# A state space scan that makes the outputs of two chunks in one run

## The chip, the cores and the metric

One NeuronCore of a Trainium2 chip runs the whole program. The metric is the device time of one execution in microseconds (us), given as the median of several runs.

## What is computed

The reference is a trunk of two layers on 2048 tokens of width 1024, in float32. The first is a state space layer (Mamba-2), the second attention over a sliding window. Only the first is touched by the change:

```python
z, xbc, dt = split(h @ w_in)                       # z: gate, xbc: x, B and C
xbc = silu(causal_depthwise_conv(xbc, conv_w, conv_b))   # 4 taps
dt = softplus(dt + dt_bias); A = -exp(a_log)
# ssd_chunked, chunks of 128 tokens, 8 groups of 4 heads of 64 channels, state 128
a_cs = cumsum(dt * A)                              # within a chunk
decay = exp(where(causal, a_cs[l] - a_cs[s], -inf))
y_diag = einsum('gls,grls,sgrp->lgrp', C @ B.T, decay, x * dt)
states = einsum('lgn,grl,lgrp->grpn', B, exp(a_cs[-1] - a_cs), x * dt)
h_in = scan over chunks of  h * exp(a_cs[-1]) + states
y_off = einsum('lgn,grpn,grl->lgrp', C, h_in, exp(a_cs))
y = (y_diag + y_off + d_skip * x) * silu(z)        # skip and gate
out = x + rmsnorm(rmsnorm(y) @ w_out)
```

## The kernel before

Float32 products are made as three products of split operands (`mm3`: high by high, low by high, high by low). The state space layer works on half the tokens at a time (1024, `hf`), and in a half on one group of heads after the other (`g`, eight of them). For each group `ssm_proj` makes twelve product tiles `ps` of 128 channels by 512 tokens: two blocks of tokens each for B, C, x0, x1 and the gates z0, z1. Each takes 24 products of 128x512, accumulated in one of four PSUM buffers (tag `pj`), and the weights of a column tile are loaded by SyncE (`wraw`), rounded by ScalarE (`whi`) and subtracted by GpSimd (`wlo`), with two buffers for each. B, C, x0 and x1 then pass the convolution: ScalarE copies the tile to `raw` and makes the last tap with the bias in `acc`, VectorE adds three taps (L747), ScalarE makes a tanh into `sx` (L750) and VectorE forms silu (L751).

Beside the products of a group runs the scan of the group before it, `ssm_scan`, a generator whose steps `interleave` sets evenly between the products: 17 steps for eight chunks. For a chunk, `stage1` transposes x0, x1 and B on TensorE and multiplies B by C (into `pt`), VectorE and ScalarE make from it `xd`, `xw`, `xh`, `bh`, `bl` and the masked decays `dec`, GpSimd `xl`; ScalarE and GpSimd turn the loaded sums `ab` into the decayed C, in place. `stage2` makes the chunk's state (`sps`, three products of 256 columns; then `hd` on GpSimd and `hn` on VectorE) and directly behind it the outputs: 8 products of 64 output channels each into `yt`, in two halves of the partitions. Each of these stands twice in the trace, as its operands are plain float32. VectorE adds the skip (L841) and GpSimd multiplies by the gate (L843), each twice per chunk on 128 columns; every two chunks the result `ysb` is stored to `yT` in DRAM. `ab` of the chunk after next is loaded behind `stage2`.

At the change of halves the next tokens are normalised and transposed (`prep`) beside the last group; behind the last group the last scan runs beside the first two token tiles of the out-projection (`first`, `head`). The order of instructions on each engine is set when the program is built: a scheduling layer of the language reorders what the code issues within its dependencies, and buffers of a pool (`bufs`) decide what waits for what. SyncE issues all loads and stores shown here, in order.

Of the kernel before, what the change touches and what calls it, by code (L numbers as in the profile page):

```python
# [37 lines left out]
AIN = 2560  # L38

# [20 lines left out]
class Trunk:  # L60
# [7 lines left out]
    def consts(self, pool):  # L68
# [3 lines left out]
        self.identr = pool.tile([P, P], F32R, name="identr")  # L72
        nc.vector.tensor_copy(self.identr, self.ident)
# [22 lines left out]
    def prep(self, src, b, wn, hs, rss=None):  # L96
        """Append (hi, lo) to hs: [k % P, k // P, t] of rmsnorm(src)[t, k] * wn."""
# [46 lines left out]
    def split_w(self, src, cols):  # L144
        """Split weights [K, cols] (k on partitions) into tiles hi, lo [P, K // P, cols]."""
# [10 lines left out]
    def rope_tables(self, wp):  # L156
        """cs2 = [cos, cos] and sn2 = [-sin, sin], [token % P, token // P, 16]."""
# [11 lines left out]
        # r = ang - 2 pi n with n = round(ang / 2 pi) and exact products  # L169
# [57 lines left out]
    def out_piece(self, st, ws, src, i, k0, nk, kt, gated):  # L227
        """k tiles k0 .. k0 + nk of the out-projection of tokens i * P .. (i + 1) * P."""
# [27 lines left out]
    def out_finish(self, st, i, xin, xout, pw, gated, rs=None):  # L256
        """xout = xin + rmsnorm(u) * pw, where u is first scaled to unit mean square of its input if gated;
        rs: [P, 1] for the inverse root mean square of xout."""
# [13 lines left out]
        if gated:  # L272
            # s = r1 * (r1^2 * mean(u^2) + eps)^-0.5 with r1 = (mean(y^2) + eps)^-0.5
# [22 lines left out]
    def att(self, ctx, x1, oT, wn, rs1, hs0, wout, sts):  # L296
# [3 lines left out]
        if True:  # L300
# [7 lines left out]
            # tril[i, j] = 1 where j <= i; mprev[j, i] = 1 where j > i  # L308
# [243 lines left out]
    def ssm_consts(self, pool):  # L552
# [16 lines left out]
        # conv weights and bias and the gate norm, halved, one channel per partition  # L569
# [16 lines left out]
    def dt_proj(self, pool, hs, tabs, atd):  # L586
        """dt, decay tables of the 8 chunks of a half."""
# [23 lines left out]
        # softplus(v) = max(v, 0) + log1p(exp(-|v|)), log1p(u) = 2 atanh(u / (2 + u))  # L611
# [24 lines left out]
        # inclusive sums along the chunk, their total, and the decays  # L636
# [15 lines left out]
        # the sums once more, to DRAM, with (chunk, group) as rows of (r, l)  # L652
# [10 lines left out]
    def ssm_proj(self, ap, hs, hf, g, res, preps, dtg, tail, start):  # L663
        """In-projection, convolution and silu of one group, 1024 tokens.

        preps: generators that make the two blocks of hs, for the first group of a half;
        dtg: what makes the half's time steps, run beside it;
        tail: what to run once the first block is used up, beside the last two column tiles;
        start: called after the first products."""
# [37 lines left out]
            # the second block is made beside the first three, B's weights are split once more  # L707
# [4 lines left out]
        for at, (name, s) in enumerate(order):  # L712
# [30 lines left out]
            acc = ap.tile([P, BLK], F32, tag="cacc", name="acc", bufs=2)  # L743
            nc.scalar.activation(acc, ps, AF.Identity, bias=self.cb[:, ct:ct + 1],  # L744
                                 scale=self.cw[:, 3, ct:ct + 1])
            for j in range(3):
                nc.vector.scalar_tensor_tensor(acc, raw[:, j:j + BLK], self.cw[:, j, ct:ct + 1],  # L747
                                               acc, ALU.mult, ALU.add)
            sx = ap.tile([P, BLK], F32, tag=name, name="sx", bufs=4 if name in ("B", "C") else 3)
            nc.scalar.activation(sx, acc, AF.Tanh)  # L750
            nc.vector.scalar_tensor_tensor(sx, sx, 1.0, acc, ALU.add, ALU.mult)  # L751
            res[name, s] = sx

    def ssm_scan(self, sp, yp, tabs, hf, g, res, yT):
# [3 lines left out]
        hprev = self.hsave[g] if hf else None  # L758
        ysb = None

        abs_ = []

        def load(c):
            ab = sp.tile([P, 4, P], F32, tag="ab", name="ab")
            j = c * 8 + g
            nc.sync.dma_start(ab.rearrange("p r l -> p (r l)"), atd[j].partition_broadcast(P))
            abs_.append(ab)

        def stage1(c):
            ab = abs_[c]  # L770
# [10 lines left out]
            xd = sp.tile([P, 4, 64], F32, tag="xd", name="xd")  # L781
# [14 lines left out]
            cbm = sp.tile([P, P], F32, tag="cbm", name="cbm")  # L796
            nc.vector.tensor_tensor(cbm, pt[:, 3, :], self.triu, ALU.mult)
            dec = sp.tile([P, 4, P], F32, tag="dec", name="dec")
# [10 lines left out]
            return xd, (bh, bl, xh, xl), dec, ce  # L809

        def stage2(c, st, hprev, ysb):
            s, o = divmod(c, 4)
            sl = slice(o * P, (o + 1) * P)
            xd, bx, dec, ce = st
            # next state
            sps = yp.tile([P, 256], F32, tag="st", name="sps")
            self.mm3(sps, *bx, True, True)
            hn = self.hsave[g] if (hf == 0 and c == 7) else sp.tile([P, 256], F32, tag="hst", name="hn")
# [7 lines left out]
            # outputs, two heads stacked on partitions  # L826
            yt = yp.tile([P, 2, P], F32, tag="y", name="yt", bufs=2)
            for pr in range(2):
                for e in range(2):
                    r = 2 * pr + e  # L830
                    nc.tensor.matmul(yt[64 * e:64 * e + 64, pr, :], xd[:, r, :], dec[:, r, :],
                                     start=True, stop=ce is None)
                if ce is not None:
                    for e in range(2):
                        r = 2 * pr + e
                        nc.tensor.matmul(yt[64 * e:64 * e + 64, pr, :], hprev[:, 64 * r:64 * r + 64], ce[:, r, :],
                                         start=False, stop=True)
            for pr in range(2):
                xx = res[f"x{pr}", s]
                yv = ysb[:, pr, (o % 2) * P:(o % 2) * P + P]  # L840
                nc.vector.scalar_tensor_tensor(yv, xx[:, sl], self.dch[:, 2 * g + pr:2 * g + pr + 1],  # L841
                                               yt[:, pr, :], ALU.mult, ALU.add)
                nc.gpsimd.tensor_tensor(yv, yv, res[f"z{pr}", s][:, sl], ALU.mult)  # L843
            return hn

        load(0)
        load(1)
        st = stage1(0)
        yield
        for c in range(8):  # L850
            s, o = divmod(c, 4)
            if o % 2 == 0:
                ysb = sp.tile([P, 2, 2 * P], F32, tag="ysb", name="ysb")
            nxt = stage1(c + 1) if c < 7 else None
            yield
            hprev = stage2(c, st, hprev, ysb)
            if c < 6:
                load(c + 2)
            st = nxt
            if o % 2 == 1:  # L860
                t0 = (8 * hf + c - 1) * P
                nc.sync.dma_start(
                    yT[2 * g * P:(2 * g + 2) * P, t0:t0 + 2 * P].rearrange("(a p) t -> p a t", p=P), ysb)
            yield

# [9 lines left out]
    def run(self, ctx):  # L875
# [9 lines left out]
        self.px = self.pool(ctx, "px", 5)  # L885
# [7 lines left out]
        self.cs2 = cp.tile([P, T // P, 16], F32, name="cs2")  # L893
        self.sn2 = cp.tile([P, T // P, 16], F32, name="sn2")

        # state space layer: y (doubled, before its norm), channel-major, to DRAM
        with ExitStack() as actx:
# [22 lines left out]
            def first(scan):  # L920
                """Beside the last column tiles: the last scan on their finished first block, weights."""
# [8 lines left out]
                for _ in range(3):  # L930
                    next(scan)
                    yield
            for hf in range(2):
                tabs = {}
                hs, hnext = hnext, []
                for g in range(NG):
# [11 lines left out]
                    interleave(self.ssm_proj(ap, hs, hf, g, res, preps, dtg, tail, start), cost, side, 17)  # L948
# [76 lines left out]
```

## Time and profile before

| | |
|---|---|
| median of 3 runs | 2611.55 us (2610.59 to 2617.84) |
| the profiled execution, first to last instruction | 2612.3 us |
| TensorE busy | 2563.8 us, 98% |
| VectorE, ScalarE, GpSimd busy | 1701.4, 1267.6 and 1085.8 us |
| state space layer, up to the end of the last scan | 0 to about 1425 us |
| its out-projection, then the attention layer and its out-projection | to about 1760 us, to 2612 us |

No time of the profiled execution beside its span is given; the span is 0.75 us above the median. A matmul's length in the trace reaches from its issue to its last result, and the next one begins before that, so that the distance from one start to the next tells more than the lengths. PE in the rows is TensorE, PEld its weight loads, DVE is VectorE, ACT ScalarE, POOL GpSimd and SPq SyncE's queue of DMA issues. L831 is line 831 of the kernel.

### The profile page before, as it was taken

The numbers are of one execution on the slowest core, as the hardware profiler recorded it, in microseconds if no ns is written. First come the engines' busy times: TensorE is split into PE (matmuls) and PEld (weight loads), VectorE is DVE, ScalarE is ACT, GpSimd is POOL, SyncE is SP. The second block draws the span as 40 slices with busy tenths as digits, with TensorE's granted clock in tenths as the row PEclk, the third lists the DMA queues.
The fourth block names the chain that finished last, engine by engine and source line by source line (L and its number), as shares of the span: only waits on it lengthen the run. The fifth ranks groups of instructions, "written<-read, shape, count | busy, mean of one in ns | idle before, by whom it ended". The sixth has DMA issues, their size and how long they took to land. (4 is left out here: it accounts for less than half of the span.)

```text
span 2612.3 us, 39548 instructions
## 1 busy us (share of the span) xinstructions
PE 2563.8 (98%) x14307; PEld 2125.4 (81%) x14307; DVE 1701.4 (65%) x3612; ACT 1267.6 (49%) x3015; POOL 1085.8 (42%) x1013
## 2 busy tenths in 40 slices
PE   7999999999999999999998999999999999999998
PEld 6878888888777888888886888888888888888787
DVE  6678666776786667766688544457666767667522
ACT  5455555555645555555556322234545555454321
POOL 2465555555455556555566322223222122221222
PEclk9999999999999999999999999999999999999999
DMA  4322222223323222222225332234112121102343
GB/s 125 106 78 73 78 80 72 88 62 88 88 73 119 71 76 81 69 80 78 80 75 175 108 97 97 97 121 136 53 53 57 58 73 53 53 27 65 105 145 121
DMA packets 266659, 224.50 MB, mean 86 GB/s; under 512 B 31136, under 2 KB 229984, under 8 KB 266464
## 3 DMA queue, kind: packets, MB, share of 16 engines
q1 hardware_dynamic: 266464, 221.98, 27.8%
q8 instruction: 113, 1.85, 0.3%
q14 instruction: 82, 0.67, 0.1%
HBM read 179.72 MB, written 42.21 MB: 85 GB/s over the span
## 5 line engine op out<-in xcount | busy, mean ns | idle before, releaser
L91 PE MATMUL ps<-hi,whi 128*128 128x512 f32 (+1 forms) x1808 | 731.4, 405 | 1.0 <-ACT hi L140 1.0
L93 PE MATMUL ps<-hi,wlo 128*128 128x512 f32 (+1 forms) x1808 | 706.8, 391 | 0.9 <-POOL wlo L153 0.9
L92 PE MATMUL ps<-lo,whi 128*128 128x512 f32 (+1 forms) x1808 | 703.1, 389 | 1.1 <-DVE lo L141 1.1
L91 PEld LDWEIGHTS ps<-hi,whi 128*128 128x128 f32 x1808 | 340.8, 189 | 79.1 <-issue 19.0
L93 PEld LDWEIGHTS ps<-hi,wlo 128*128 128x128 f32 x1808 | 340.4, 188 | 76.9 <-POOL wlo L153 1.7
L92 PEld LDWEIGHTS ps<-lo,whi 128*128 128x128 f32 x1808 | 341.7, 189 | 61.0 <-DVE lo L141 1.8
L747 DVE SCALAR_TENSOR_TENSOR acc<-raw,cw,acc 128x512 f32<-128x512 f32 x384 | 344.5, 897 | 21.8 <-ACT acc L744 17.3
L153 POOL TENSOR_TENSOR wlo<-wraw,whi 128x1024 fp32r<-128x1024 f32 x114 | 282.5, 2478 | 133.7 <-ACT whi L151 121.8
L800 ACT ACTIVATE dec<-ab,acs 128x128 f32<-128x128 f32 x512 | 167.3, 392 | 172.1 <-DMA ab<-atd 165.5
L806 POOL TENSOR_TENSOR ab<-ab,sx 128x512 f32<-128x512 f32 x120 | 162.9, 1358 | 195.3 <-ACT ab L805 189.4
L252 PE MATMUL u<-oh,yh 128*128 128x512 f32 x768 | 241.6, 394 | 0.0
L252 PE MATMUL u<-ol,yh 128*128 128x512 f32 x768 | 239.3, 392 | 0.0
L252 PE MATMUL u<-oh,yl 128*128 128x512 f32 x768 | 238.2, 390 | 0.0
L377 POOL TENSOR_TENSOR qs<-qf,qs 128x256 fp32r<-128x256 f32 x64 | 49.3, 770 | 419.2 <-ACT qs L376 387.9
L750 ACT ACTIVATE sx<-acc 128x512 f32<-128x512 f32 x128 | 81.0, 633 | 268.1 <-DVE acc L747 267.9
L236 POOL TENSOR_TENSOR yl<-yr,yh 128x1024 fp32r<-128x1024 f32 (+1 forms) x64 | 118.9, 1858 | 164.9 <-ACT yh L234 164.9
L843 POOL TENSOR_TENSOR ysb<-ysb,zz 128x128 f32<-128x128 f32 x256 | 162.6, 648 | 48.9 <-DVE ysb L841 48.1
L91 PE MATMUL ps<-qh,hi 128*128 128x384 f32 x512 | 177.7, 348 | 0.0
L92 PE MATMUL ps<-ql,hi 128*128 128x384 f32 x512 | 172.9, 338 | 0.9 <-POOL ql L333 0.9
L93 PE MATMUL ps<-qh,lo 128*128 128x384 f32 x512 | 172.3, 337 | 0.0
L252 PEld LDWEIGHTS u<-oh,yl 128*128 128x128 f32 x768 | 144.2, 188 | 32.1 <-issue 0.9
L234 ACT ACTIVATE yh<-yr 128x1024 fp32r<-128x1024 f32 (+1 forms) x64 | 54.1, 846 | 238.7 <-PE u L252 176.4
(217 smaller groups left out, 4827.9 us busy)
## 6 DMA issues: line engine op xcount, KB each, us to landing
wraw<-in_ssm_w_in SPq DMA_DIRECT2D x98, 512.0 KB, 4.0
ab<-atd SPq DMA_DIRECT2D x128, 256.0 KB, 3.2
xt<-in_x SPq DMA_DIRECT2D x32, 512.0 KB, 5.0
yT<-ysb SPq DMA_DIRECT2D x64, 256.0 KB, 2.2
yr<-yT SPq DMA_DIRECT2D x32, 512.0 KB, 4.0
xt<-x SPq DMA_DIRECT2D x32, 512.0 KB, 4.0
oraw<-in_ssm_w_out SPq DMA_DIRECT2D x16, 512.0 KB, 5.9
x<-xt SPq DMA_DIRECT2D x32, 256.0 KB, 2.1
```

What stands on the lines that cost most here:

```text
L91: nc.tensor.matmul(ps, sh, mh, start=first, stop=False)
L92: nc.tensor.matmul(ps, sh, ml, start=False, stop=False)
L93: nc.tensor.matmul(ps, sl, mh, start=False, stop=last)
L153: nc.gpsimd.tensor_tensor(lo, raw, hi.bitcast(F32), ALU.subtract)
L234: nc.scalar.activation(yh, yr, AF.Copy)
L236: nc.gpsimd.tensor_tensor(yl, yr, yh.bitcast(F32), ALU.subtract)
L252: nc.tensor.matmul(st["u"][h], y[:, k, :], w[:, j, 512 * h:512 * h + 512], start=k0 + k == 0 and m == 0, stop=k0 + k == kt - 1 and m == 2)
L747: nc.vector.scalar_tensor_tensor(acc, raw[:, j:j + BLK], self.cw[:, j, ct:ct + 1], acc, ALU.mult, ALU.add)
L750: nc.scalar.activation(sx, acc, AF.Tanh)
L800: nc.scalar.activation(dec[:, r, :], ab[:, r, :], AF.Relu, scale=-1.0, bias=acs[:, c, 4 * g + r:4 * g + r + 1])
L806: nc.gpsimd.tensor_tensor(ce, ce, Ct[:, sl].unsqueeze(1).to_broadcast([P, 4, P]), ALU.mult)
L843: nc.gpsimd.tensor_tensor(yv, yv, res[f"z{pr}", s][:, sl], ALU.mult)
```

## The change

The scan goes by pairs of chunks. `stage2` is divided into `state`, for one chunk, and `outputs`, for two. A pair's steps are: the state of the first chunk with `stage1` two chunks ahead; the same for the second; then the outputs of both into one `yt` of 256 columns, with one skip and one gate for each half of the heads, the store, and the loads of two `ab`. That makes 14 steps. `ab`, `xd` and `dec` get four buffers instead of two, `hn` three, `cbm` one. The convolution accumulates in `sx` itself and puts the tanh into `raw`, so that `acc` is gone. The pool `px` has four buffers instead of five, and the rope tables and `identr` are made in a pool of their own behind the state space layer.

```diff
+SCAN = 14
-            acc = ap.tile([P, BLK], F32, tag="cacc", name="acc", bufs=2)
-            nc.scalar.activation(acc, ps, AF.Identity, bias=self.cb[:, ct:ct + 1],
+            sx = ap.tile([P, BLK], F32, tag=name, name="sx", bufs=4 if name in ("B", "C") else 3)
+            nc.scalar.activation(sx, ps, AF.Identity, bias=self.cb[:, ct:ct + 1],
                                  scale=self.cw[:, 3, ct:ct + 1])
             for j in range(3):
-                nc.vector.scalar_tensor_tensor(acc, raw[:, j:j + BLK], self.cw[:, j, ct:ct + 1],
-                                               acc, ALU.mult, ALU.add)
-            sx = ap.tile([P, BLK], F32, tag=name, name="sx", bufs=4 if name in ("B", "C") else 3)
-            nc.scalar.activation(sx, acc, AF.Tanh)
-            nc.vector.scalar_tensor_tensor(sx, sx, 1.0, acc, ALU.add, ALU.mult)
+                nc.vector.scalar_tensor_tensor(sx, raw[:, j:j + BLK], self.cw[:, j, ct:ct + 1],
+                                               sx, ALU.mult, ALU.add)
+            th = raw[:, 0:BLK]
+            nc.scalar.activation(th, sx, AF.Tanh)
+            nc.vector.scalar_tensor_tensor(sx, th, 1.0, sx, ALU.add, ALU.mult)
             res[name, s] = sx
...
-            xd = sp.tile([P, 4, 64], F32, tag="xd", name="xd")
+            xd = sp.tile([P, 4, 64], F32, tag="xd", name="xd", bufs=4)
...
-            dec = sp.tile([P, 4, P], F32, tag="dec", name="dec")
+            dec = sp.tile([P, 4, P], F32, tag="dec", name="dec", bufs=4)
...
+        def outputs(c0, hps):
+            yt = yp.tile([P, 2, 2 * P], F32, tag="y", name="yt", bufs=2)
+            for u in range(2):
+                xd, _, dec, ce = sts[c0 + u]
+                for pr in range(2):
+                    yo = yt[:, pr, u * P:(u + 1) * P]
                     for e in range(2):
                         r = 2 * pr + e
+                        nc.tensor.matmul(yo[64 * e:64 * e + 64], xd[:, r, :], dec[:, r, :],
+                                         start=True, stop=ce is None)
+                    if ce is not None:
+                        for e in range(2):
+                            r = 2 * pr + e
+                            nc.tensor.matmul(yo[64 * e:64 * e + 64], hps[u][:, 64 * r:64 * r + 64], ce[:, r, :],
+                                             start=False, stop=True)
+            s, o = divmod(c0, 4)
+            sl = slice(o * P, (o + 2) * P)
+            ysb = sp.tile([P, 2, 2 * P], F32, tag="ysb", name="ysb")
             for pr in range(2):
+                yv = ysb[:, pr, :]
+                nc.vector.scalar_tensor_tensor(yv, res[f"x{pr}", s][:, sl], self.dch[:, 2 * g + pr:2 * g + pr + 1],
                                                yt[:, pr, :], ALU.mult, ALU.add)
                 nc.gpsimd.tensor_tensor(yv, yv, res[f"z{pr}", s][:, sl], ALU.mult)
...
+        for c in range(0, 8, 2):
+            h0 = hprev
+            h1 = state(c, h0)
+            stage1(c + 2)
             yield
+            hprev = state(c + 1, h1)
+            stage1(c + 3)
             yield
+            outputs(c, (h0, h1))
+            load(c + 4)
+            load(c + 5)
+            yield
...
-        self.px = self.pool(ctx, "px", 5)
+        self.px = self.pool(ctx, "px", 4)
```

What this moves is read from the written order of both programs. On TensorE, in the middle of a group, the order before has the state of a chunk (`sps`) and its outputs (`yt`) between the products `ps` of the next group:

```order
L93 MATMUL ps<-hi,wlo 128x512
L91 MATMUL sps<-xh,bh 128x256
L92 MATMUL sps<-xl,bh 128x256
L93 MATMUL sps<-xh,bl 128x256
L831 MATMUL yt<-dec,xd 64x128 x2
L836 MATMUL yt<-ab,hn 64x128 x2
L831 MATMUL yt<-dec,xd 64x128 x2
L836 MATMUL yt<-ab,hn 64x128 x2
L91 MATMUL ps<-hi,whi 128x512
```

After the change, at the same place of a group, the outputs of two chunks stand between products `ps`:

```order
L92 MATMUL ps<-hi,wlo 128x512
L833 MATMUL yt<-dec,xd 64x128 x2
L838 MATMUL yt<-ab,hn 64x128 x2
L833 MATMUL yt<-dec,xd 64x128 x2
L838 MATMUL yt<-ab,hn 64x128 x2
L833 MATMUL yt<-dec,xd 64x128 x2
L838 MATMUL yt<-ab,hn 64x128 x2
L833 MATMUL yt<-dec,xd 64x128 x2
L838 MATMUL yt<-ab,hn 64x128 x2
L90 MATMUL ps<-hi,whi 128x512
```

And 18 to 24 products away from them stands the state of one chunk, followed by the transposes of the chunk two further:

```order
L91 MATMUL sps<-xl,bh 128x256
L92 MATMUL sps<-xh,bl 128x256
L776 MATMUL pt<-ident,sx 128x128
L777 MATMUL pt<-ident,sx 128x128
L778 MATMUL pt<-ident,sx 128x128
L779 MATMUL pt<-sx 128x128
L90 MATMUL ps<-hi,whi 128x512
```

Over the whole program the `yt` products stand in 129 runs before and in 66 after (64 pairs, one of them cut into three at the change of halves); `sps` is followed directly by a product of another tile, `ps` or `u`, 8 times before and 31 times after. The number of products is the same. On SyncE's queue, in the steady part of the second half, the order before is (`ab`: decay sums, `wraw`: weights, `yT`: the stored outputs)

```order
L766 DMA ab<-atd_60 128x512
L862 DMA yT<-ysb 128x2x256
L766 DMA ab<-atd_60 128x512
L149 DMA wraw<-in_ssm_w_in 128x8x128
L766 DMA ab<-atd_60 128x512
L862 DMA yT<-ysb 128x2x256
L149 DMA wraw<-in_ssm_w_in 128x8x128
```

and after the change

```order
L148 DMA wraw<-in_ssm_w_in 128x8x128
L764 DMA ab<-atd_60 128x512 x2
L849 DMA yT<-ysb 128x2x256
L148 DMA wraw<-in_ssm_w_in 128x8x128 x2
L764 DMA ab<-atd_60 128x512
```

so that a weight load stands behind two loads of `ab` and a store instead of one or two of these. The ScalarE row of the convolution that writes `sx` for the second block of `x0` (L743 after the change) waits there for VectorE, and the decays of the next two chunks stand behind it.

## Rows read from the trace of the kernel before

**Rows 1.** The page: the span, and section 1, busy time of each engine
```profile
span 2612.3 us, 39548 instructions
...
PE 2563.8 (98%) x14307; PEld 2125.4 (81%) x14307; DVE 1701.4 (65%) x3612; ACT 1267.6 (49%) x3015; POOL 1085.8 (42%) x1013
```

**Rows 2.** Busy time by stage; columns: stretch, length, busy of each engine (instructions)
```profile
200.00:1360.00 1160.00, 1152.27 (x6626) 943.36 (x6626) 826.51 (x1606) 633.57 (x1363) 651.12 (x615) 1.00 0.27 79
...
1425.00:1760.00 335.00, 335.00 (x1494) 275.51 (x1491) 158.59 (x252) 109.80 (x164) 99.24 (x77) 1.00 0.34 109
```

**Rows 3.** TensorE's timeline around one chunk's outputs; columns: start, length, what
```profile
505.89 0.40 PE L93 MATMUL ps<-hi,wlo 128*128 128x512 f32 x1
...
507.94 0.39 PE L93 MATMUL ps<-hi,wlo 128*128 128x512 f32 x1
...
508.28 0.28 PE L92 MATMUL sps<-xl,bh 128*128 128x256 f32 x1
508.40 0.28 PE L93 MATMUL sps<-xh,bl 128*128 128x256 f32 x1
508.61 0.44 PE L831 MATMUL yt<-dec,xd 128*64 128x128 f32 x4
508.88 0.39 PE L836 MATMUL yt<-ab,hn 128*64 128x128 f32 x4
509.10 0.39 PE L831 MATMUL yt<-dec,xd 128*64 128x128 f32 x4
509.31 0.39 PE L836 MATMUL yt<-ab,hn 128*64 128x128 f32 x4
509.63 0.50 PE L91 MATMUL ps<-hi,whi 128*128 128x512 f32 x1
509.97 0.40 PE L92 MATMUL ps<-lo,whi 128*128 128x512 f32 x1
...
511.82 0.39 PE L91 MATMUL ps<-hi,whi 128*128 128x512 f32 x1
```

**Rows 4.** Groups of instructions by shape; columns: count | busy us, mean ns | idle before, releasers
```profile
L843 POOL TENSOR_TENSOR ysb<-ysb,zz 128x128 f32<-128x128 f32 x256 | 162.6, 648 | 48.9 <-DVE ysb L841 48.1
...
L831 PE MATMUL yt<-dec,xd 128*64 128x128 f32 x1024 | 105.6, 286 | 11.8 <-DVE dec L808 8.7 <-DVE ysb L841 3.0
...
L836 PE MATMUL yt<-ab,hn 128*64 128x128 f32 x896 | 87.9, 273 | 0.0
L824 POOL TENSOR_TENSOR hd<-hn,cd 128x256 f32<-128x256 f32 x104 | 87.2, 839 | 120.3 <-DVE hn L825 76.8 <-DVE raw L739 21.2 <-DVE raw L737 19.6
...
L841 DVE SCALAR_TENSOR_TENSOR ysb<-sx,dch,yt 128x128 f32<-128x128 f32 x256 | 80.1, 339 | 19.7 <-PE yt L836 18.6 <-PE yt L831 1.0
...
L287 DVE SCALAR_TENSOR_TENSOR v<-u,s,bc 128x512 f32<-128x512 f32 x64 | 45.1, 747 | 11.2 <-POOL s L87 10.7
...
L836 PE MATMUL yt<-ab,hsave 128*64 128x128 f32 x64 | 6.8, 291 | 0.0
```

**Rows 5.** Timelines of SyncE's queue and of ScalarE: a weight load and its conversion
```profile
502.69 0.37 SPq L149 DMA_DIRECT2D wraw<-in_ssm_w_in  x1
...
522.31 1.06 ACT L151 ACTIVATE whi<-wraw 128x1024 fp32r<-128x1024 f32 x1 [0.36 <-issue]
```

**Rows 6.** TensorE's waits from 0 to 1370 us; columns: total, times, longest
```profile
PE yt L831 <- DVE dec L808: 4.9, 2, 3.4
PE yt L831 <- DVE ysb L841: 3.0, 2, 1.8
...
PE sps L91 <- DVE hn L825: 1.2, 2, 0.6
```

**Rows 7.** TensorE's waits from 1370 to 1426 us, the last scan
```profile
PE yt L831 <- DVE dec L808: 3.8, 3, 2.4
PE sps L91 <- ACT bh L793: 2.2, 2, 2.0
PE sps L92 <- POOL xl L791: 2.0, 3, 1.5
```

More of the change, by code (lines that the diff above doesn't have):

```diff
@@ L757, in ssm_scan @@
         dt, acs, cd, w2, atd = (tabs[k] for k in ("dt", "acs", "cd", "w2", "atd"))
-        hprev = self.hsave[g] if hf else None
-        ysb = None
-        abs_ = []
+        abs_, sts = [], []
         def load(c):
[L764 to L767, printed above, removed]
+            if c < 8:
+                ab = sp.tile([P, 4, P], F32, tag="ab", name="ab", bufs=4)
+                j = c * 8 + g
+                nc.sync.dma_start(ab.rearrange("p r l -> p (r l)"), atd[j].partition_broadcast(P))
+                abs_.append(ab)
         def stage1(c):
+            if c > 7:
+                return
             ab = abs_[c]
@@ L808, in stage1, with state @@
             nc.vector.tensor_tensor(dec, dec, cbm.unsqueeze(1).to_broadcast([P, 4, P]), ALU.mult)
[L809 to L814, printed above, removed]
+            sts.append((xd, (bh, bl, xh, xl), dec, ce))
+        def state(c, hprev):
             sps = yp.tile([P, 256], F32, tag="st", name="sps")
-            self.mm3(sps, *bx, True, True)
-            hn = self.hsave[g] if (hf == 0 and c == 7) else sp.tile([P, 256], F32, tag="hst", name="hn")
+            self.mm3(sps, *sts[c][1], True, True)
+            hn = self.hsave[g] if (hf == 0 and c == 7) else sp.tile([P, 256], F32, tag="hst", name="hn", bufs=3)
             if hprev is None:
@@ L825, in stage2 @@
                 nc.vector.tensor_tensor(hn, hd.rearrange("p h d -> p (h d)"), sps, ALU.add)
[L827 to L833, printed above, removed]
+            return hn
+        def outputs(c0, hps):
[4 more added lines that the diff above has]
+                    yo = yt[:, pr, u * P:(u + 1) * P]
@@ L842, in stage2 @@
                                                yt[:, pr, :], ALU.mult, ALU.add)
                 nc.gpsimd.tensor_tensor(yv, yv, res[f"z{pr}", s][:, sl], ALU.mult)
[L844 to L848, printed above, removed]
-        yield
[L850 to L854, printed above, removed]
-            yield
[L856 to L863, printed above, removed]
+            t0 = (8 * hf + c0) * P
@@ new lines, in outputs @@
+            nc.sync.dma_start(
+                yT[2 * g * P:(2 * g + 2) * P, t0:t0 + 2 * P].rearrange("(a p) t -> p a t", p=P), ysb)
+        for c in range(4):
+            load(c)
+        stage1(0)
+        yield
+        stage1(1)
+        yield
+        hprev = self.hsave[g] if hf else None
+        for c in range(0, 8, 2):
+            h0 = hprev
+            h1 = state(c, h0)
+            stage1(c + 2)
+            yield
+            hprev = state(c + 1, h1)
+            stage1(c + 3)
+            yield
+            outputs(c, (h0, h1))
+            load(c + 4)
+            load(c + 5)
@@ L892, in run @@
         self.gn = cp.tile([P, 16], F32, name="gn")
-        self.cs2 = cp.tile([P, T // P, 16], F32, name="cs2")
-        self.sn2 = cp.tile([P, T // P, 16], F32, name="sn2")
         with ExitStack() as actx:
@@ L929, in first @@
                     yield
-                for _ in range(3):
-                    next(scan)
-                    yield
+                next(scan)
+                yield
             for hf in range(2):
@@ L947, in run @@
                     cost = 56 if g == 0 else 52 if hf and g == NG - 1 else 58
-                    interleave(self.ssm_proj(ap, hs, hf, g, res, preps, dtg, tail, start), cost, side, 17)
+                    interleave(self.ssm_proj(ap, hs, hf, g, res, preps, dtg, tail, start), cost, side, SCAN)
                     if dtg:
@@ L963, in head @@
                 yield from pieces[1]
-            interleave(head(), 15, side, 10)
+            interleave(head(), 15, side, SCAN - 5)
         wn = self.bcast(cp, io["pre_norm"][1], tag="wn")
         rs1 = cp.tile([P, T // P], F32, name="rs1")
+        rope = self.pool(ctx, "rope")
+        self.cs2 = rope.tile([P, T // P, 16], F32, name="cs2")
+        self.sn2 = rope.tile([P, T // P, 16], F32, name="sn2")
+        self.identr = rope.tile([P, P], F32R, name="identr")
+        nc.vector.tensor_copy(self.identr, self.ident)
         hs = []
```

9 lines of the change are left out of this document (1 added, 8 removed).

## The prediction

> **What bounds the kernel now.** I read the page first, then the busy times by stage, then TensorE's timeline inside one stage, then its waits. The page gives a span of 2612.3 us with TensorE busy 98% of it [rows 1]. By stages the change touches only the state space layer, up to about 1425 us; there TensorE is busy 1152.27 of 1160 us in the long middle, while VectorE has 827, ScalarE 634 and GpSimd 651 us [rows 2]. TensorE's stream sets the time, and of the others only what it waits for counts. That stream is not simply full, though. In the timeline [rows 3] one should look at starts, not durations: a 128x512 product lasts 0.39 to 0.40 us, but the next one starts 0.228 us later (507.94 less 505.89, over nine products). Up to 0.16 us can therefore be lost between two products without any idle time being shown. That is what the rows from 508.28 to 509.97 show, when the scan's small products cut into the stream.
>
> **The price of one run of outputs.** A run means the 64-column products into `yt` that follow each other with nothing else between them. Its price is read from [rows 3] in five places. (1) Entry: `sps` products start 0.12 apart, the first `yt` starts 0.21 after the last `sps`: 0.09 lost. (2) The rows with x4 are a quarter of the run each; the second and third take 0.22 and 0.21, the first 0.27 (508.61 to 508.88): 0.05 lost. (3) Exit: the last quarter takes 0.32 until the next `ps` starts (509.31 to 509.63): 0.105 lost. (4) That `ps` is followed 0.34 later instead of 0.228: 0.11 lost. (5) The eight after it take 1.85 us (509.97 to 511.82) instead of 1.82: 0.03. Together 0.385 us, paid per run however long it is, since the quarters in between go at an even pace.
>
> **The change part by part.**
>
> *Outputs of two chunks together.* In the written order 129 runs become 66; the shapes and the number of the products stay ([rows 4]: 1024 records of L831, 896 of L836 and 64 more on the saved state). 63 runs fewer, at 0.385: 24.3 us gained. One piece of this has no row: the entry will mostly come from a 128x512 product, not from `sps`. I take the same 0.09. The bounds are nothing lost there, and a wait for the whole 0.39 us that such a product lasts, thus 0.39 - 0.228 = 0.16. The 129 old runs cost 49.7 us; 66 new ones cost 66 x 0.295 = 19.5 or 66 x 0.455 = 30.0, so the gain is 30.2 at best and 19.7 at worst. The Trainium skill, "TensorEngine Tiling (Array Packing)", section "Tiling Modes", says that changing the tiling mode, and not just the tile, drains the engine. Taken strictly, the entry would wait for the product before it to be finished, the gain would be 4.6 us smaller and the time 2590 instead of 2585. The trace does not bear out the strict reading: `yt` enters 0.21 us after an `sps` that lasts 0.28.
>
> *The state product now stands with the next chunk's transposes, or alone.* `sps` followed by transposes pays nothing new: the transposes' own exit is there before and after. At the end of a scan there is no chunk left to transpose, and `sps` then returns to `ps` by itself: by the order 23 more such returns. The trace has hardly any of them; the nearest rows are items 4 and 5 above, 0.14 us, so 3.3 us lost, bounds 0 and 23 x 0.25 = 5.8 (with an exit like item 3).
>
> *Skip and gate on 256 columns.* VectorE's skip took 339 ns for 128 columns, and the like operation on 512 columns, also from PSUM, 747 [rows 4]; by a straight line between them 475 for 256. 256 x 0.339 becomes 128 x 0.475: 26 us less on VectorE. GpSimd's gate, 256 x 0.648, becomes 128 at some 0.84 (the row of `hd`, 256 columns): 58 us less. Neither engine is full [rows 2], so I put nothing down for it; their earlier ends show in the waits below. If VectorE were the limit the gain would be up to 26 us.
>
> *Convolution in place.* The same number of instructions on the same shapes; what moves is which buffer waits. `raw` is held to the last step (the old `acc` was, with two buffers as well), and `sx` is taken when the first step is written, some 4 us sooner. That makes one new wait: ScalarE's L743 for the second block of `x0` writes where the scan still reads chunks 2 and 3, whose skip comes by the order 12 products (2.7 us) and a run (some 1.9 us) later, plus two skips of 0.475. So ScalarE stands some 6 us once per group. Behind it are the decays of the next chunks and the next evacuation, which TensorE wants three product tiles later: 3 x 24 x 0.228 = 16 us. The wait is hidden with 10 us to spare, so 0.
>
> *Loads.* `ab` is fetched in pairs, and each weight load on SyncE's queue stands behind a pair and a store of `yT`. Weights have room: the load issued at 502.69 us is first read by ScalarE at 522.31 [rows 5], 20 us later. A group's 288 products take 66 us, so with the scan's own a chunk is some 9 to 10 us, and a delay by one chunk stays covered: 0. One `px` buffer fewer and the rope tables moved out of the way touch the out-projections, where TensorE shows 335.00 of 335.00 us busy [rows 2]; a token tile's input would have to come 22 us (96 x 0.228) late before that cover is gone: 0.
>
> *Waits.* TensorE's waits in the scan sum to 9.1 us before 1370 us [rows 6] and 8.0 us in the last scan [rows 7]. The 4.9 us on `dec` are the first outputs of a half, which now come some 54 products after the transposes instead of 15: gone. Of the 4.2 us on the freed `yt` and on `hn` I take back a quarter, as both buffers stay as few. The last scan keeps its 8.0: nine steps stand between fewer products of the out-projection, with fewer runs. 6 us gained; bounds 17.1 gained and 10 lost.
>
> *Sum*, against the profiled execution's 2612.3 us: less 24.3, plus 3.3, less 6.0 gives 2585.3. The median of the runs is 0.75 us lower, so 2585 us, 1.0% less.
>
> **The rivals.** *TensorE is full: only waits can be won.* For it speaks the busy time of 99% in the middle stage [rows 2]; then the lost time at a run's ends would be the small products' own and be paid at other ends, and the time is 2612.3 + 3.3 - 6 or so, 2600 to 2612. Against it are the equal quarters inside the run [rows 3]. The Trainium skill, "Perfetto Trace Analysis", section "Identifying the Most-Contended Engine", calls TensorE's busy share a poor measure of headroom since matmuls are pipelined, and points to the share of weight loads. Here that is 943 of 1160 us [rows 2], which by it leaves room, and the trace agrees.
>
> *The last scan stalls more.* Its two states and the pair's outputs stand six products apart (1.4 us), and the chain from transposes through VectorE, ScalarE and GpSimd to `xl` already ends late there [rows 7]. If each of the three pairs left there waits 4 us more, 12 us go back: 2597.
>
> *Slower: ScalarE's new wait uncovers PSUM.* The four product buffers give 16 us. If the wait on chunks 2 and 3 lasted 20 us instead of 6, each of 15 groups would lose about 4 us, 60 in all, less the 27: 2645. It decides from 16 + 27/15 = 18 us on. Nothing in the waits of before [rows 6] comes near it.
>
> *More than forecast:* all 17.1 us of waits gone and free entries: 2612 - 30 - 17 + 3 = 2568.
>
> That the order does not do what is written is excluded by the order itself, but for one place at the change of halves where a run is cut into three (counted above).
>
> **How the numbers follow.** Forecast (2572 to 2599) 0.66; full TensorE 0.16; last scan 0.08; slower 0.05; more 0.05. A measurement tells about 0.3%, 8 us, from no change, so faster means below 2603.7: 0.66 + 0.07 + 0.05 and a quarter of the full-TensorE case, 0.82. Within: 0.13. Slower: 0.05. The range 2570 to 2605 leaves out most of the full-TensorE case, the slower one and a little below.
>
> **What would show it.** In the profile after: the same counts of `yt` records, in 66 runs, with edges of 0.09, 0.05, 0.105, 0.11 and 0.03 us as before; the stage from 200 to 1360 us shorter by some 20 us at the same work; no waits on `dec` in the first scan of a half; the attention layer unchanged. I am wrong if runs of 32 cost twice the edges of runs of 16, if the entry from `ps` costs 0.16 us more, or if TensorE waits for `ps` buffers or weights in every group.

## The result, and the profile after

The changed kernel takes 2684.5 us (2682.9 to 2687.0, four runs) against 2611.1 us in the runs beside it: 1.0273 times the time, interval 1.026 to 1.0286. Forecast were 2585 us and faster; it is slower by 2.7%. One of the ten runs of e8 below took 9350.7 us at a granted clock of 0.50; the ratios leave it out. The page of the changed kernel, span and section 1:

```profile
span 2681.2 us, 39280 instructions
...
PE 2570.6 (96%) x14307; PEld 2142.0 (80%) x14307; DVE 1707.9 (64%) x3484; ACT 1266.6 (47%) x3015; POOL 1051.0 (39%) x885
```

Against [rows 1] TensorE runs the same 14307 instructions, but it is idle for 2681.2 - 2570.6 = 110.6 us instead of 48.5, and busy for 6.8 us more, where 21 less were expected. Both need a cause. First the edges of a run of outputs, in TensorE's timeline (start, length, what), to be held against [rows 3]:

```profile
499.47 0.39 PE L92 MATMUL ps<-hi,wlo 128*128 128x512 f32 x1
499.79 0.44 PE L833 MATMUL yt<-dec,xd 128*64 128x128 f32 x4
500.06 0.39 PE L838 MATMUL yt<-ab,hn 128*64 128x128 f32 x4
...
501.37 0.39 PE L838 MATMUL yt<-ab,hn 128*64 128x128 f32 x4
501.68 0.50 PE L90 MATMUL ps<-hi,whi 128*128 128x512 f32 x1
502.02 0.40 PE L91 MATMUL ps<-lo,whi 128*128 128x512 f32 x1
```

The entry from a 128x512 product takes 0.32 us from start to start (0.228 + 0.09), the first quarter 0.27, the exit 0.31, the product behind it 0.34, and the quarters between go at an even pace. These are the prices of the prediction, now paid once for two chunks. So the gain is there, and something else took more. TensorE's waits from 0 to 1500 us (total, times, longest):

```profile
PE sps L90 <- DVE hn L821: 74.1, 19, 7.2
```

In [rows 6] this wait had 1.2 us, twice; the waits of `yt` on `dec` and on `ysb` of [rows 6] are gone. One group of the first half shows what it is. Timelines (start, length, engine, what, and the idle time before with its releaser), TensorE first, then SyncE's queue, ScalarE, VectorE and GpSimd:

```profile
505.89 0.28 PE L90 MATMUL sps<-xh,bh 128*128 128x256 f32 x1
...
510.69 0.39 PE L92 MATMUL ps<-hi,wlo 128*128 128x512 f32 x1
515.00 0.55 PE L90 MATMUL sps<-xh,bh 128*128 128x256 f32 x1 [3.92 <-DVE hn L821]
...
503.67 0.37 SPq L148 DMA_DIRECT2D wraw<-in_ssm_w_in  x1
504.13 1.00 SPq L764 DMA_DIRECT2D ab<-atd  x2
...
504.69 0.78 ACT L743 ACTIVATE sx<-ps,cb,cw 128x512 f32<-128x512 f32 x1 [1.84 <-DVE ysb L845]
508.74 1.57 ACT L800 ACTIVATE dec<-ab,acs 128x128 f32<-128x128 f32 x5 [3.28 <-DMA ab<-atd]
510.23 0.57 ACT L739 ACTIVATE raw<-ps 128x512 f32<-128x512 f32 x1
510.70 0.76 ACT L743 ACTIVATE sx<-ps,cb,cw 128x512 f32<-128x512 f32 x1
...
505.50 2.88 DVE L746 SCALAR_TENSOR_TENSOR sx<-raw,cw,sx 128x512 f32<-128x512 f32 x3 [0.46 <-ACT sx L743]
511.50 0.75 DVE L746 SCALAR_TENSOR_TENSOR sx<-raw,cw,sx 128x512 f32<-128x512 f32 x1 [0.50 <-ACT sx L743]
512.77 1.76 DVE L746 SCALAR_TENSOR_TENSOR sx<-raw,cw,sx 128x512 f32<-128x512 f32 x1
514.45 0.41 DVE L821 TENSOR_TENSOR hn<-hd,sps 128x256 f32<-128x256 f32 x1
...
512.58 1.40 POOL L806 TENSOR_TENSOR ab<-ab,sx 128x512 f32<-128x512 f32 x1 [6.32 <-ACT ab L805]
```

Read it backwards. The second state of the pair starts at 515.00, when `hn` of the first, which reads the only `sps` buffer, has run (514.45). `hn` stands on VectorE behind two taps of a convolution tile (511.50 and 512.77, the second 1.76 us long, beside GpSimd's decayed C, L806, late with the same pair of `ab`). Their `raw` and `sx` come from ScalarE at 510.23 and 510.70, behind `dec` of a later chunk, and that waited for `ab` until 508.74. `ab` was issued at 504.13, behind a weight load that had itself waited; and ScalarE had stood 1.84 us for the second block of `x0` before. The first state ran at 505.89, so `hn` came 9.0 us behind its state, while the next state is wanted after 18 products `ps`, 5.2 us (515.00 - 3.92 - 505.89). In the steady groups this happens once per group, at the third pair: some 4 us in the first half, 5 to 7 in the second.

The wait costs more than itself. Busy times by stretch of the same place; the third column from the right is the granted clock:

```profile
505.00:511.00 6.00, 6.00 (x31) 4.84 (x29) 3.02 (x5) 2.72 (x8) 1.26 (x2) 1.00 0.76 216
511.00:514.95 3.95, 0.08 (x1) 0.00 (x0) 3.45 (x5) 3.92 (x9) 1.42 (x2) 0.92 0.00 0
514.95:521.00 6.05, 6.00 (x18) 5.16 (x19) 6.05 (x9) 3.45 (x7) 6.05 (x5) 0.50 0.00 0
521.00:525.00 4.00, 4.00 (x25) 3.05 (x26) 4.00 (x10) 0.58 (x2) 1.53 (x2) 0.98 0.46 131
```

TensorE is called busy from 514.95 to 521, but at 0.50, its lower level of 1.2 GHz: 18 instructions in 6.05 us, against 31 in 6.00 before the wait. From the first product of `sps` to the twelfth `ps` behind it the stalled place takes 6.4 us (515.00 to 521.38), the first state of the same pair 3.4 (505.89 to 509.33): about 2.9 us more per such wait, hidden in the busy time.

### The profile page after: what moved, and what is told of

Same layout as the page of the kernel before. It is cut to its first block, busy times and chain, and to the rows that moved or that the text cites. A ratio compares the mean times of both kernels' runs of the same rounds, so it can differ in the third digit from the quotient of the medians.

```text
span 2681.2 us, 39280 instructions
## 1 busy us (share of the span) xinstructions
PE 2570.6 (96%) x14307; PEld 2142.0 (80%) x14307; DVE 1707.9 (64%) x3484; ACT 1266.6 (47%) x3015; POOL 1051.0 (39%) x885
## 4 chain that ended last, share of the span: by engine, by line
PE 71%; DVE 10%; DMA 5%; ACT 5%; issue 4%; POOL 4%; SPq 0%; ACTq 0%; POOLq 0%; DVEq 0%
PE u L251 18%; PE ps L90 13%; PE ps L91 13%; PE ps L92 13%; DMA ab<-atd 4%; DVE sx L746 4%; PE sc L421 2%; POOL wlo L152 2%; PE yt L833 2%; PE yt L838 1%; PE ot L467 1%; ACT dec L800 1%; PE tt L449 1%; PE tq L388 1%; PE ot L471 1%
## 5 line engine op out<-in xcount | busy, mean ns | idle before, releaser
L746 DVE SCALAR_TENSOR_TENSOR sx<-raw,cw,sx 128x512 f32<-128x512 f32 x384 | 378.0, 985 | 20.2 <-ACT sx L743 17.5
L800 ACT ACTIVATE dec<-ab,acs 128x128 f32<-128x128 f32 x512 | 168.1, 392 | 170.8 <-DMA ab<-atd 160.5
L806 POOL TENSOR_TENSOR ab<-ab,sx 128x512 f32<-128x512 f32 x120 | 166.8, 1390 | 184.5 <-ACT ab L805 181.2
L749 ACT ACTIVATE raw<-sx 128x512 f32<-128x512 f32 x128 | 80.6, 630 | 294.3 <-DVE sx L746 275.6
L847 POOL TENSOR_TENSOR ysb<-ysb,zz 128x256 f32<-128x256 f32 x128 | 111.2, 886 | 153.8 <-DVE ysb L845 153.8
L251 PEld LDWEIGHTS u<-ol,yh 128*128 128x128 f32 x768 | 144.1, 188 | 31.4 <-DVE ol L223 0.7
```

Source lines behind the costliest of these rows:

```text
L251: nc.tensor.matmul(st["u"][h], y[:, k, :], w[:, j, 512 * h:512 * h + 512], start=k0 + k == 0 and m == 0, stop=k0 + k == kt - 1 and m == 2)
L746: nc.vector.scalar_tensor_tensor(sx, raw[:, j:j + BLK], self.cw[:, j, ct:ct + 1], sx, ALU.mult, ALU.add)
L749: nc.scalar.activation(th, sx, AF.Tanh)
L800: nc.scalar.activation(dec[:, r, :], ab[:, r, :], AF.Relu, scale=-1.0, bias=acs[:, c, 4 * g + r:4 * g + r + 1])
L806: nc.gpsimd.tensor_tensor(ce, ce, Ct[:, sl].unsqueeze(1).to_broadcast([P, 4, P]), ALU.mult)
```

## The experiments

Theory A: the second state of a pair has come to stand one step behind the first and waits for its `hn`, which goes behind a convolution tile on VectorE; what makes that tile late (the load of `ab`, its place behind a weight load, the wait for `x0`) adds up. The rivals are that one of these is the cause by itself. All ratios are against the kernel before on the same chip (median 2611.1 us beside the changed kernel, 2614.8 beside the first four runs, 2614.4 beside the next four, 2615.3 beside the last three). TensorE's times and the waits are of one profiled run each.

| run | us | ratio and interval | TensorE busy, idle, us | waits of `sps` on `hn`, us |
|---|---|---|---|---|
| before | 2611.1 | | 2563.8, 48.5 | 1.2 |
| changed | 2684.5 | 1.0273 (1.026 to 1.0286) | 2570.6, 110.6 | 74.1 |
| e1_state_pair | 2685.3 | 1.0263 (1.0244 to 1.0281) | 2572.6, 110.6 | 73.8 |
| e2_ab_five | 2641.0 | 1.0095 (1.0076 to 1.0113) | 2562.0, 79.0 | 45.3 |
| e3_x0_four | 2649.2 | 1.0132 (1.0109 to 1.0154) | 2561.6, 92.7 | 26.3, and 29.8 put down to `dec` |
| e4_weights_other_queue | 2633.0 | 1.0067 (1.0046 to 1.0087) | 2551.2, 79.3 | 36.6 |
| e5_queue_and_ab_five | 2638.3 | 1.0091 (1.0076 to 1.0106) | 2557.1, 81.9 | 41.6 |
| e6_pause_between_states | 2596.1 | 0.9933 (0.9918 to 0.9948) | 2543.1, 48.7 | 10.7 |
| e7_second_state_other_bank | 2628.0 | 1.0054 (1.0038 to 1.0071) | 2552.4, 72.9 | 16.7 |
| e8_in_place_alone | 2618.1 | 1.0012 (1.0003 to 1.0022) | 2565.2, 47.8 | 0.6 |
| e9_pause_behind_outputs | 2678.8 | 1.0255 (1.0238 to 1.0272) | 2562.9, 111.0 | 70.8 |
| e10_queue_ab_x0 | 2607.1 | 0.9976 (0.9967 to 0.9985) | 2544.9, 62.8 | 23.3 |
| e11_pause_and_room | 2592.2 | 0.9921 (0.9904 to 0.9938) | 2539.1, 48.2 | 10.3 |

**Two halves of one tile for a pair's states.**

```diff
-            sps = yp.tile([P, 256], F32, tag="st", name="sps")
+            if c % 2 == 0:
+                stp.append(yp.tile([P, 2, 256], F32, tag="st", name="sps"))
+            sps = stp[-1][:, c % 2, :]
```

> The changed kernel, but the two states of a pair have the two halves of one PSUM tile, so that the second state needn't wait until VectorE has read the first. Theory A (the stall of each group is the second state waiting for the one PSUM buffer of `sps`, which VectorE reads late): the waits of `sps` on `hn`, 74.1 us in the changed kernel, fall below 15 us, TensorE's clock stays up, and the time is 2585 to 2600 us, as the gain at the edges of the runs is then bare. Rival B (the scan as a whole is late, since its inputs are): the stall moves on to the next products of the scan, `yt` or the next pair's `sps`, and the time stays above 2650 us.

Nothing moved, and the trace names the same releaser:

```profile
PE sps L90 <- DVE hn L823: 73.8, 19, 6.3
```

In this kernel's written order too the second state's first product waits for a VectorE instruction. So the edit didn't part the two states, and the run tells nothing of what a buffer of its own would bring; e7 asks that again.

**One contributor at a time.** A fifth buffer for `ab` (room from `ysb`):

```diff
-                ab = sp.tile([P, 4, P], F32, tag="ab", name="ab", bufs=4)
+                ab = sp.tile([P, 4, P], F32, tag="ab", name="ab", bufs=5)
-            ysb = sp.tile([P, 2, 2 * P], F32, tag="ysb", name="ysb")
+            ysb = sp.tile([P, 2, 2 * P], F32, tag="ysb", name="ysb", bufs=1)
```

> The changed kernel with five buffers of `ab` instead of four (and one `ysb` instead of two, to make room). The load of a pair's first chunk no longer waits for the outputs of the pair before. Theory A, with the late `ab` as what starts the chain (ScalarE waits for it, VectorE's taps wait for ScalarE, `hn` stands behind the taps, the second state waits for `hn`): at least half of the 74.1 us of waits of `sps` goes and with it half of the slow clock, so 2610 to 2645 us. Rival C (what starts it is ScalarE's wait for the buffer of the second block of x0): nothing changes, 2680 to 2690 us.

A fourth buffer for `x0`, with the same room:

```diff
-            sx = ap.tile([P, BLK], F32, tag=name, name="sx", bufs=4 if name in ("B", "C") else 3)
+            sx = ap.tile([P, BLK], F32, tag=name, name="sx", bufs=4 if name in ("B", "C", "x0") else 3)
```

> The changed kernel with four buffers for x0 instead of three (and one `ysb` instead of two, to make room). The convolution of the second block of x0 no longer waits for the skip of chunks 2 and 3. Rival C: the stall in each group goes, 2590 to 2620 us. Theory A with the late `ab` at its start: ScalarE only waits for `ab` instead, and the time stays at 2675 to 2690 us.

The weights issued by GpSimd instead of SyncE:

```diff
-        nc.sync.dma_start(raw, src.rearrange("(k p) c -> p k c", p=P))
+        nc.gpsimd.dma_start(raw, src.rearrange("(k p) c -> p k c", p=P))
```

> The changed kernel with the weight loads of a column tile issued by GpSimd instead of SyncE. A pair of `ab` then no longer stands behind a weight load that waits for its buffer; in the trace of the changed kernel that was 2.4 us in the group looked at (501.7 to 504.13 us). Theory A with SyncE's order as the reason why `ab` is late: the stalls become 2 us shorter each, 2630 to 2660 us, if the issue itself costs GpSimd little. If `ab` is late because of its buffers and its own 4 us to land, the time moves by less than 10 us, 2675 to 2690 us.

Each took back a part, 44, 35 and 52 us of 73, and in different places. With five `ab` the second half's waits fell to about 1 us a group and the first half's only to 3.4; with four `x0` the first half's fell to about 2 and the second half's stayed near 5. The profile puts six of the second half's down to `dec`, but there too `hn` ends 0.15 us before the state starts, as in the others, so they count as waits for `hn`. The times with five `ab` and with the other queue lie in theory A's ranges, though five `ab` took only 28.8 us of the waits, less than the half expected; 2649 with four `x0` lies between the two ranges given, so neither the late `ab` nor the wait for `x0` is the cause by itself. That 44, 35 and 52 sum to more than the 73 fits links of one chain better than separate costs. None alone brings the kernel to the time before.

**Queue and `ab` together.**

> Weights fetched by GpSimd's queue and a fifth buffer for ab (one for ysb), both together. Alone they gave 2633 and 2641 us against 2685 of the changed kernel. Theory A (all of it is one chain: late ab, ScalarE, the taps on VectorE, hn, the second state; each piece shortens it): together they take the chain below the 5 us that a step leaves, the second state waits under 10 us in all, granted clock back to 0.995, time 2590 to 2610. Rival (both take away the same microseconds of the load): no more than the better one alone, 2625 to 2640.

The rival's number came: 2638, no better than the queue alone. ScalarE's waits for `ab` had fallen from 160.5 us to 14.1, and still the first half waited 3.0 us a group. What stands there on VectorE and GpSimd:

```profile
504.65 4.29 DVE L746 SCALAR_TENSOR_TENSOR sx<-raw,cw,sx 128x512 f32<-128x512 f32 x3 [0.46 <-ACT sx L743]
...
504.91 1.09 POOL L847 TENSOR_TENSOR ysb<-ysb,zz 128x256 f32<-128x256 f32 x1
505.97 1.27 POOL L806 TENSOR_TENSOR ab<-ab,sx 128x512 f32<-128x512 f32 x1
507.21 1.18 POOL L847 TENSOR_TENSOR ysb<-ysb,zz 128x256 f32<-128x256 f32 x1
```

Three taps take 4.3 us beside three GpSimd instructions in a row, where a tap mostly takes 0.74. The pair's outputs bring two gates of 256 columns at once, and they fall on the taps that stand before `hn`: a fourth contributor. In the changed kernel the same three taps took 2.88 us (505.50), since GpSimd's decayed C (L806), held up by the late `ab`, ran only at 512.58. An earlier `ab` puts it between the gates and onto these taps, so part of what the load gives is taken back.

**An empty step between the states.**

```diff
-SCAN = 14
+SCAN = 18
             h1 = state(c, h0)
             stage1(c + 2)
             yield
+            yield
             hprev = state(c + 1, h1)
```

> One empty step between the two states of a pair, 18 steps a group instead of 14, all else as in the changed kernel: the states of a pair stand two steps (some 9 us) apart instead of one (some 6 us). Theory A (the second state waits for the hn of the first, which is late behind the convolution; the lateness itself, some 10 us from state to hn, was there before as well): the wait is covered up to 9 us, 3 to 4 us of each stall go in the first half and 4 of 6 in the second; 2590 to 2615. Rival (the loads stall the engines and TensorE pays wherever it stands): the stalls move but stay, 2650 to 2685.

2596 us, 0.7% faster than before. The same place of a group, TensorE and VectorE:

```profile
489.36 0.28 PE L90 MATMUL sps<-xh,bh 128*128 128x256 f32 x1
499.22 0.28 PE L90 MATMUL sps<-xh,bh 128*128 128x256 f32 x1
...
497.94 0.41 DVE L821 TENSOR_TENSOR hn<-hd,sps 128x256 f32<-128x256 f32 x1
```

`hn` is as late as in the changed kernel, 9.0 us from the state's start to its own end. But the next state now stands 9.9 us away, and TensorE doesn't wait. (In the second half `hn` also came earlier, at most 7 us behind its state in the steady groups instead of 10 to 12, so that there it isn't the distance alone.) One part of the expectation was wrong: that this lateness had been there before the change. Before, at the latest `hn` of a steady group:

```profile
499.15 0.28 PE L91 MATMUL sps<-xh,bh 128*128 128x256 f32 x1
508.17 0.28 PE L91 MATMUL sps<-xh,bh 128*128 128x256 f32 x1
...
503.80 0.41 DVE L825 TENSOR_TENSOR hn<-hd,sps 128x256 f32<-128x256 f32 x1
```

That is 5.1 us of lateness against 9.0 of distance. The change did both: it made `hn` later and brought the next state nearer.

**The second state in another bank.** In six of eight groups it takes one of the four product buffers:

```diff
-            sps = yp.tile([P, 256], F32, tag="st", name="sps")
+            sps = (self.pp.tile([P, 256], F32, tag="pj", name="sps") if c % 2 and g < 6
+                   else yp.tile([P, 256], F32, tag="st", name="sps"))
```

> In six of eight groups the second state of a pair goes to one of the four product buffers instead of the one buffer of the states, so that it needn't wait until VectorE has read the first. Theory A (the one buffer of sps is what TensorE stops at): 12 of 16 stalls go, what waits next is the outputs a step later, for hn; 2600 to 2630. Rival (ScalarE and VectorE are late for all that TensorE wants, so that the next product buffer isn't free either): the wait comes back within 3 us at ps or at sps itself, with three buffers left for the products; 2665 to 2700.

In a middle group of the first half, TensorE and VectorE:

```profile
479.43 0.28 PE L90 MATMUL sps<-xh,bh 128*128 128x256 f32 x1
484.45 0.28 PE L90 MATMUL sps<-xh,bh 128*128 128x256 f32 x1
...
489.68 0.40 DVE L822 TENSOR_TENSOR hn<-hd,sps 128x256 f32<-128x256 f32 x1
```

The second state starts 5.0 us behind the first, before `hn` has run, and nothing waits. From 200 to 600 us the list of TensorE's waits is empty. That shows that the one buffer of `sps` is what TensorE stopped at. In the second half other waits come in its place (0 to 1500 us):

```profile
PE sps L91 <- POOL xl L791: 10.7, 6, 2.1
...
PE yt L839 <- DVE hn L822: 6.0, 4, 2.0
PE ps L92 <- POOL wlo L152: 5.4, 7, 1.8
```

GpSimd and `hn` are now what comes next; the 16.7 us on `hn` in the table lie in the groups that keep the one buffer and in the last scan. So the time, 2628, is in the range of theory A, at its upper end.

**The convolution in place, alone,** in the kernel before (the diff is the convolution's part of the change).

> The kernel before with nothing but the convolution in place. By the prediction's step the new wait of ScalarE for the second block of x0 is covered: 2611 to 2618, no stall of TensorE over 1 us that was not there. Rival (the wait itself costs, as the 35 us that a fourth buffer for x0 gave back in the changed kernel could mean): 2640 or more. Theory A says that it costs only together with the two states one step apart, so it sides with the first.

2618 us, 1.0012 times before: nothing to speak of. With the states 8 to 10 us apart the new wait is covered.

**The control: the empty step behind the outputs.**

```diff
             load(c + 4)
             load(c + 5)
             yield
+            yield
```

> The control to the pause between the states: the same 18 steps a group, but the empty step stands behind the outputs and loads of a pair, so that the two states stand one step of 4.8 us apart instead of 6.2, and the loads of ab come a step ahead of their use. Theory A (what counts is the distance from a state to the next against the 9 to 10 us that hn takes): the load's share of the lateness goes, as with five buffers for ab (2641), but the step is 1.4 us shorter in each of 16 groups; second states still wait in every group, 2630 to 2670. Rival (it is the number of steps, or the load alone, that the pause cured): 2595 to 2610.

The same 18 steps give 2679 us, 9 above theory A's range and far from the rival's. The waits come twice a group. Their sum, the two states of one pair, and the `hn` between them:

```profile
PE sps L90 <- DVE hn L821: 70.8, 35, 4.0
...
482.65 0.28 PE L90 MATMUL sps<-xh,bh 128*128 128x256 f32 x1
487.87 0.36 PE L90 MATMUL sps<-xh,bh 128*128 128x256 f32 x1 [1.40 <-DVE hn L821]
...
487.32 0.41 DVE L821 TENSOR_TENSOR hn<-hd,sps 128x256 f32<-128x256 f32 x1
```

Without the wait the two states are only 3.8 us apart here, and 3.3 at the pair behind (12 products `ps` instead of 18), less than the 4.8 that the expectation put down. ScalarE's waits for `ab` were 66.3 us instead of 160.5, so the loads did come earlier, and `hn` with them: 5 to 7 us behind its state in the first half instead of 9. The shorter distance took that back. It is the distance against the lateness that counts, not the number of steps.

**Everything that feeds the chain, in the order of the changed kernel** (three buffers for C make the room).

> Weights on GpSimd's queue, five buffers for ab and four for x0 (one for ysb, three for C), with the order of the changed kernel. In the run with the first two VectorE's taps of one tile took 4.3 us beside GpSimd's gates and decayed C instead of 2.2, and the first half kept a wait of 3.1 us per group; a fourth x0 buffer lets ScalarE write that tile before the outputs, away from the gates. Theory A (the lateness of hn is a sum of all three): the first half's waits fall under 1.5 us, 2600 to 2622. Rival (hn is late by its place behind two tiles of the convolution alone, whatever feeds them): no better than 2633 to 2640.

2607 us, in theory A's range: the contributors do add up, and with these three eased the 14 steps are about as fast as before (0.2% less). 1.4 us a group stay in the first half, where `hn` is 6.4 us late against 5.2 of distance.

**The pause, and all that room.**

> The pause between the states (2596 us, with six waits of 10.7 us in all left), and with it weights on GpSimd's queue, five buffers for ab and four for x0. If what is left there is the load and the x0 wait at the ends of the halves, 3 to 6 us more are gained: 2590 to 2594. If the rest is the shape of the half's ends, nothing: 2594 to 2599. Over 2600 would say that the weights' issues cost GpSimd's stream more than they bring.

2592 us, 0.8% less than before and the best of all; its interval overlaps with that of the pause alone.

## Why the prediction was wrong

*Outputs of two chunks together: right in size. The returns of `sps`: nothing instead of 3.3 us.* The sum was 24.3 - 3.3 = 21.0 us less TensorE time. In e6, where idle time is as before (48.7 against 48.5 us), TensorE's busy time is 2563.8 - 2543.1 = 20.7 us lower. That the two agree so closely is partly luck. A return of `sps` to `ps`, in the changed kernel:

```profile
530.66 0.28 PE L91 MATMUL sps<-xl,bh 128*128 128x256 f32 x1
530.78 0.28 PE L92 MATMUL sps<-xh,bl 128*128 128x256 f32 x1
530.90 0.40 PE L90 MATMUL ps<-hi,whi 128*128 128x512 f32 x1
531.13 0.39 PE L91 MATMUL ps<-lo,whi 128*128 128x512 f32 x1
```

The starts are 0.12, 0.12 and 0.23 us apart, so nothing is lost. And TensorE is busy at a granted clock of 0.50 for 17.3 us in e6 and for 9.6 before. A 128x512 product then starts 0.427 us behind the last (517.27 to 521.11, nine products) instead of 0.228, so the difference of 7.7 us hides some 3.6. Without it e6 is 24.3 us lower and, by the same working with 70.9 us at 0.50, the changed kernel 21.7: near the 24.3 put on the runs alone. The strict reading of the Trainium skill, "TensorEngine Tiling (Array Packing)", section "Tiling Modes", would have cost 0.07 us more per entry; the entry of 0.32 us doesn't show it. The rival of the full TensorE falls too: 20.7 us of busy time could be won.

*The step that failed* stands in the same part: it priced the runs and not what the merging does to the states. The text said where the state of the next chunk stands, 18 to 24 products away, and took only the product that follows it into account. It did not ask what the next state waits for: one `sps` buffer, read by `hn`. Before, 8 to 10 us lay between two states; in a pair there are 5, while `hn` comes 9 us behind its state. "Of the 4.2 us on the freed `yt` and on `hn` I take back a quarter" is where the sum has it, as a gain. It became 74.1 us of waits and, behind them, the lower clock.

*Convolution in place: 0 was right by itself (e8) and wrong here.* The list of what stands behind ScalarE's waiting instruction ended too early. Behind it are the decays and the next evacuation, as written, but behind that evacuation are VectorE's taps, and behind these `hn`. The cover was not the 16 us of product buffers but the distance of the states. ScalarE's wait itself was smaller than the 6 us put down: 1.84 in the group shown, 20.9 us in 14 times over 0 to 1500 us, 4.6 at most.

*Loads: 0 was wrong.* The prediction followed what stands behind the `ab` pair, the weights. It missed what the pair stands behind: a weight load that waits for its buffer. ScalarE's waits for `ab` from 0 to 1500 us, before and after:

```profile
ACT dec L800 <- DMA ab<-atd: 165.5, 64, 5.8
...
ACT dec L800 <- DMA ab<-atd: 160.5, 66, 7.1
```

The same sum, free then and on the path now.

*Skip and gate.* The skip fell by 24.4 us (80.1 in [rows 4] to 55.7) and the gate by 51.4 (162.6 to 111.2), near the 26 and 58 put down. But VectorE's total rose by 6.5 us, since the taps went from 344.5 to 378.0 us (0.897 to 0.985 each). In e8, with the convolution in place but no pairs, a tap takes 0.869, so the pairing does it; e5 shows one such place. In the changed kernel the 154 taps that overlap GpSimd's work by no more than 0.1 us take 0.74 us on average, the other 230 take 1.15. The Trainium skill, "SBUF — State Buffer", section "Who interferes with whom", says that a VectorE instruction with two SBUF inputs contends with a GpSimd one that reads SBUF. The taps and gates are such a pair, and the 1.15 us beside GpSimd agree. The prediction left this out.

*The slower rival* had the wrong end: it looked at the product buffers, priced at 2645 with a chance of 0.05. TensorE never waited for them; the wait in every group that was to prove the prediction wrong came at `sps`. *The rival of the last scan* did not come: TensorE waits 8.0 us there (1370 to 1500 us), as before, though 6.1 of it is now on `hn`.

*The account:* 2612.3 us before, less 20.7 for the runs, plus 62.1 of idle time (110.6 - 48.5), plus 27.5 of busy time that the changed kernel has over e6, which runs the same products with few waits. That makes 2681.2, the span, as it must, since 20.7 and 27.5 both come from e6. But the 27.5 can be held against the clock: the changed kernel is busy at 0.50 for 70.9 us, e6 for 17.3. At 0.427 instead of 0.228 us for a product the difference of 53.6 us is worth some 25, nearly all of it. Of the 68.9 us by which the span grew, 64.2 are there at the end of the last scan: its last state starts at 1424.3 us before and at 1488.5 after. The attention layer, from TensorE's first product into `tk` to the end, takes 819.4 and 820.6 us, unchanged as put down.

What stays open: how much of the lateness of `hn` is the taps beside GpSimd and how much the late `ab`, the weight load ahead of it and `x0`. Each was taken away in some run, but never the GpSimd part alone.

## What to carry to other kernels

When work is regrouped, list for every buffer with one copy how far its next writer has moved towards its last reader, in time, and hold that against how late this reader runs. A reader on an engine that takes its instructions in order is as late as the slowest thing queued ahead of it, through every engine that feeds that. Where the merged work gains something, keep the distance with an empty step before adding buffers: the empty step gave back 88 us here.

## What the hardware showed besides

A wait of TensorE of 3.9 us was followed by 6 us at half clock (0.50, 2.9 us lost); in e10, whose waits in the middle of the first half last 1.4 us, stretches of 7 us around them show a granted clock of 1.00. In e4 six groups of the first half wait 1.8 us each; behind two of these waits (499.63 and 667.37 us) the granted clock is 0.76 on the mean of 7 us, behind the other four 1.00. So these runs don't tell from which length of wait on the clock falls. It fits that e9, with 70.8 us of waits in 35 pieces, has 7.7 us less busy time than the changed kernel with 74.1 us in 19.
